# The last up group of an FFN by the seven-product form, in a fused streaming-encoder step

## The chip, the cores and the metric

The kernel runs on one core of one Trainium2 chip. The metric is device time in microseconds (us) of one execution; less is better. Engines are named as the profile names them: PE (TensorE matmul), PEld (its weight loads), DVE (VectorE), ACT (ScalarE), POOL (GpSimd) and SP (SyncE, which here only issues DMAs).

## What is computed

One layer of a hybrid streaming encoder for two groups of requests that share the weights: a convolution branch and an attention branch, mixed, and behind them a gated feed-forward network (FFN). The change touches the FFN alone. 256 prompt frames and 8 x 16 frames of running streams make 384 tokens, three tiles of 128.

```
    h2 = rmsnorm(x, norm_ffn_g)
    up = h2 @ w_up                       # (384, 2048) @ (2048, 11264)
    g_half = up[..., :D_FF]              # D_FF = 5632
    u_half = up[..., D_FF:]
    ext_f = jnp.concatenate([ffn_buf.astype(g_half.dtype), g_half], axis=1)
    gc = causal_dwconv(ext_f, ffn_dw_w, ffn_dw_b)          # 3 taps along time
    x = x + (jax.nn.silu(gc) * u_half) @ w_down            # (384, 5632) @ (5632, 2048)
    new_ffn = ext_f[:, -(FFN_CONV_W - 1):]
```

All of it is float32. TensorE works in a rounded 32-bit form (fp32r), so every operand is split into a rounded part and a rest, `hi` and `lo`, and every product is three matmuls: hi times hi, hi times lo, lo times hi.

## The kernel before

**Groups.** The 5632 columns of the FFN are cut into 11 groups of 512. "Up" of a group makes 512 gate and 512 value columns for 384 tokens from 16 chunks of 128 input rows. "Down" of a group (a down round, numbered by its group from 0) multiplies the gated result, four chunks of 128, by four panels of 512 output columns and adds the panels to `y`. `FFN_PLAN` (lines 192 to 195) is the order: up 0, then up g and down g-1 for g from 1 to 10, then down 10. So the end of the program is up 9, down 8, up 10, down 9, down 10.

**Steps.** Everything in the FFN is a list of steps. A step takes one weight tile of 128 x 1024 floats (two input chunks by 512 columns, 512 KB). SP loads it into one of five raw buffers: three tiles `raw` and two thirds of a fixed tile `raws`, in rotation (`stream_tile`, line 141). ACT casts it to `hi`, DVE subtracts to `lo` (there are three pairs of buffers), and PE multiplies. `step` (line 1228) records PE's matmuls of one step, and beside them the cast and subtraction for the step two further on. `room` counts free raw buffers; `load_ahead` issues loads while there are any.

**Two forms of up.** The direct form (`plain_up`, line 1473; `tokens`, line 1449) has 16 steps of 18 matmuls (2 chunks x 3 token tiles x 3). The seven-product form (`wino`, line 1380) multiplies two of the token tiles by 12 of the 16 chunks as a 2 x 2 x 2 block scheme with seven products in place of eight. It has 25 steps: 9 of 12 matmuls ("s" and "b"), 4 of 18 ("cg" and "cu", the four chunks outside the scheme) and 6 pairs of 9 and 6 ("t"). For each pair DVE first combines two raw tiles: three subtractions of 128 x 512 for its first step and a fourth for its second. The sums of token tiles that the scheme needs lie in `sums` and in a tile `late`, made once. `WINO` (line 196) names the groups in this form: 1 to 9. Groups 0 and 10 are direct.

**Turn and gating.** When a group's rows stand in `gr` (gate) and `ur` (value), `finish_up` (line 1307) turns them: DVE transposes 32 x 32 blocks of the three token tiles into a buffer `tb`, and 16 DMAs for each of `gr` and `ur`, 8 issued by SP and 8 by POOL, move the blocks into a tile `uT` (class `Turn`, line 1266). `tb` and `uT` exist once, so `ur` waits for `gr` to have left them. From the turned gate rows ACT makes four copies and two halo copies into `extf` and the first convolution tap, DVE the taps two and three (`sg`), and ACT applies SiLU. DVE multiplies the turned value rows by it (`uT<-uT,sg`, two halves), ACT casts them (`hi` part of `act`), DVE subtracts (`lo` part, `act<-uT,act`). `act` of a group is what its down round multiplies. The halves are halves of the 32-token blocks, so each holds a part of all four chunks of `act`.

**What sets the order.** A planner in the program's own Python keeps for each engine a time of its own (`now`) and a list of open work (`todo`). Work of the turn and gating goes into the gaps between a step's fixed instructions when its planned end is no later than the step's end plus `SLACK` (0.8 us). The instruction streams of the engines keep that order: DVE, ACT, SP and POOL each run theirs in order. `foresee` and `spare` compute numbers that nothing uses.

In the profile, line 1100 is the call through which all of these instructions of DVE, ACT, SP and POOL go, so they are told apart by tile. Lines 1376, 1377 and 1378 are the three matmuls of a product.

Of the kernel before, what the change touches and what calls it, by code (L numbers as in the profile page):

```python
# [15 lines left out]
P = 128  # L16
DM = 2048
NT = 384
# [23 lines left out]
def hybrid_step(  # L42
# [28 lines left out]
    made = [0, 0, -1]  # L71
# [136 lines left out]
    for what, g in FFN_PLAN:  # L208
# [22 lines left out]
        else:  # L231
            for cols in N_COLS:
                planned(w_down, 4 * g[0], cols, 4 * len(g))
# [872 lines left out]
    MM, HI, LO, SUM, RAWS, SLACK = 0.227, 1.05, 1.22, 0.7, 5, 0.8  # L1106
# [55 lines left out]
    def load_ahead():  # L1162
        while plan:
# [31 lines left out]
    at = [0]  # L1195
    need = []

    def foresee():
        behind = 0.0
        for what, g in FFN_PLAN:  # L1200
            if what == "up" and g in WINO:
                n = len(need)
                for kind, _ in WINO_STEPS:
                    if kind == "t":
                        need.extend([(9, 3 * SUM + LO), (6, SUM + LO)])
                    else:
                        need.append((18 if kind[0] == "c" else 12, LO))
                need[n] = (need[n][0], need[n][1] + behind)
                need[-2] = (need[-2][0], need[-2][1] + 0.7)
                need[-1] = (need[-1][0], need[-1][1] + 1.4)  # L1210
                behind = 2.1
            else:
                n, rounds, adds = (8, 2, 0.0) if what == "up" else (2 * len(g), 4, 2.1)
                for _ in range(rounds):
                    need.extend([(18, LO + behind)] + [(18, LO)] * (n - 1))
                    behind = adds
        need.extend([(18, 0.0)] * 2)

    def spare(end):
        latest, t, used = end + 9.0, end, 0.0  # L1220
        for j in range(at[0] + 2, min(at[0] + 14, len(need))):
            t += MM * need[j - 1][0]
            if j > at[0] + 2:
                used += LO if j == at[0] + 3 else need[j][1]
            latest = min(latest, t - 0.5 - used)
        return latest

    def step(mults, products):

        t = now["PE"]  # L1230
        for e in todo:
# [20 lines left out]
        if nxt:  # L1252
            work("DVE", hi_done + 0.1)
# [7 lines left out]
        for e in ("SP", "ACT", "DVE", "ACT", "SP"):  # L1261
            work(e, end + SLACK)
        at[0] += 1
        now["PE"] = end

    class Turn:

        def __init__(self, tiles, rows):
            self.tiles, self.rows = tiles, rows

        def one(self, t):
            if t == 0:
                self.tb = p_f.tile([P, 4, 4, NTT, 32], F32, tag="tb", bufs=1, name="tb")
            V.transpose(self.tb[:].rearrange("p q m t j -> p t m q j")[:, t],
                        getattr(self.tiles, self.rows)[:, t, :].rearrange("p (m q j) -> p m q j", m=4, q=4))
# [8 lines left out]
        def blocks(self):  # L1284
            return [("DVE", 0.72, 0.2, lambda t=t: self.one(t)) for t in range(NTT)]

        def moves(self):
            return [("SP", 1.4, 0.0 if a < 3 else 6.0, lambda a=a: self.move(a)) for a in range(4)]
# [18 lines left out]
    def finish_up(g, tiles, ready, both=True):  # L1307
        gt, ut = Turn(tiles, "gr"), Turn(tiles, "ur")
# [19 lines left out]
        def halves(x):  # L1328
# [246 lines left out]
```

## Time and profile before

| what | value |
|---|---|
| time, median of 3 runs | 1964.83 us (1963.3 to 1965.12) |
| the profiled execution's own time | 1964.78 us |
| span of the profile, first to last instruction | 1963.1 us |
| granted TensorE clock, mean | 0.999 |
| PE busy | 1951.5 us (99%), 9210 matmuls |
| DVE busy | 1448.3 us (74%) |
| ACT busy | 869.7 us (44%) |
| share of the chain that ended last on PE | 94% |

The page of the profile gives busy times by engine and by group of instructions. The timeline of an engine gives each instruction's start, its duration and, in brackets, how long the engine sat idle before it and what released it. A row with "x3" is three instructions that follow each other, with their time together. In a timeline a step of the direct form is 18 matmuls, and up of one group begins where the operand changes from `act` to `xg`.

### The profile page before, as it was taken

To read this page: it belongs to the slowest core of one execution; us is meant where nothing else is said; L and a number is where in the kernel's file an instruction comes from. 1 tells how busy PE (TensorE), PEld (TensorE's weight loads), DVE (VectorE), ACT (ScalarE), POOL (GpSimd) and SP (SyncE) were. 2 spreads that over 40 slices of the span, in tenths; PEclk is the share of its full clock that TensorE was granted. 3 is DMA by queue.
4 is the path that set the end of the run, shared out by engine and by line. 5 is a ranking of instruction groups with operands and counts; after the bars stand their busy time and mean duration, and the time that the engine had idled before them with its cause. 6 is when DMAs were issued, how large, how long until landed. Compare 5 with 4: busy or idle time off the path is not lost.

```text
span 1963.1 us, 25493 instructions
## 1 busy us (share of the span) xinstructions
PE 1951.5 (99%) x9210; PEld 1644.6 (84%) x9210; DVE 1448.3 (74%) x1977; ACT 869.7 (44%) x1212; POOL 150.4 (8%) x298
## 2 busy tenths in 40 slices
PE   9999999999999999999999999999999999999999
PEld 9888999888888888888888888888888888888887
DVE  4456879788764578677587878787878787878555
ACT  5535354433334523344454444454444445454442
POOL 2000011100000000000111010101010101010110
PEclk9999999999999999999999999999999999999999
DMA  6574777454444333644566666666666666666553
GB/s 186 150 183 118 215 168 154 138 143 132 131 130 128 128 126 122 197 132 140 156 218 202 198 203 201 199 207 195 207 189 211 194 209 190 216 189 215 146 163 114
DMA packets 242755, 335.86 MB, mean 171 GB/s; under 512 B 60651, under 2 KB 106406, under 8 KB 242620
## 3 DMA queue, kind: packets, MB, share of 16 engines
q1 hardware_dynamic: 235427, 324.21, 56.0%
q0 software_dynamic: 7168, 10.00, 1.9%
q8 instruction: 72, 1.18, 0.3%
q14 instruction: 56, 0.45, 0.1%
q10 hardware_dynamic: 32, 0.01, 0.0%
HBM read 309.45 MB, written 7.86 MB: 162 GB/s over the span
## 4 chain that ended last, share of the span: by engine, by line
PE 94%; DVE 4%; issue 1%; DMA 1%; ACT 1%; SPq 0%; ACTq 0%; DVEq 0%
PE bank L1377 17%; PE bank L1378 17%; PE bank L1376 16%; PE acc L314 8%; PE acc L312 8%; PE acc L313 8%; PE misc L314 4%; PE misc L313 4%; PE misc L312 4%; PE acc L307 2%; PE acc L309 2%; PE acc L308 2%; DVE lo L1100 1%; DVE raw L1100 0%; ACT hi L1100 0%
## 5 line engine op out<-in xcount | busy, mean ns | idle before, releaser
L168 DVE TENSOR_TENSOR lo<-raw,hi 128x1024 fp32r<-128x1024 f32 (+2 forms) x219 | 259.3, 1184 | 198.8 <-ACT hi L167 193.6
L167 ACT CAST hi<-raw 128x1024 fp32r<-128x1024 f32 (+2 forms) x219 | 221.7, 1012 | 396.6 <-PE misc L314 305.0
L1100 ACT CAST hi<-raw 128x1024 fp32r<-128x1024 f32 x207 | 217.4, 1050 | 327.2 <-PE bank L1378 273.3
L1100 DVE TENSOR_TENSOR lo<-raw,hi 128x1024 fp32r<-128x1024 f32 x207 | 252.4, 1221 | 114.7 <-ACT hi L1100 111.8
L1377 PE MATMUL bank<-lo,xg 128*128 128x512 f32 x696 | 271.9, 391 | 1.5 <-DVE lo L1100 1.5
L1376 PE MATMUL bank<-hi,xg 128*128 128x512 f32 x696 | 270.9, 389 | 0.0
L1378 PE MATMUL bank<-hi,xg 128*128 128x512 f32 x696 | 270.8, 389 | 0.0
L1100 ACT CAST hi<-raws 128x1024 fp32r<-128x1024 f32 x136 | 143.4, 1054 | 215.4 <-PE bank L1378 182.2
L1100 DVE TENSOR_TENSOR lo<-raws,hi 128x1024 fp32r<-128x1024 f32 x136 | 166.0, 1221 | 80.2 <-ACT hi L1100 77.8
L1376 PE MATMUL bank<-hi,act 128*128 128x512 f32 x528 | 205.4, 389 | 0.0
L1377 PE MATMUL bank<-lo,act 128*128 128x512 f32 x528 | 205.4, 389 | 0.0
L1378 PE MATMUL bank<-hi,act 128*128 128x512 f32 x528 | 205.4, 389 | 0.0
L312 PE MATMUL acc<-hi,hT 128*128 128x512 f32 (+1 forms) x512 | 193.2, 377 | 0.1
L314 PE MATMUL acc<-hi,hT 128*128 128x512 f32 (+1 forms) x512 | 190.7, 372 | 0.1
L313 PE MATMUL acc<-lo,hT 128*128 128x512 f32 (+1 forms) x512 | 190.4, 372 | 0.0
L1377 PEld LDWEIGHTS bank<-lo,xg 128*128 128x128 f32 x696 | 130.6, 188 | 32.5 <-DVE lo L1100 5.6
L829 DVE SCALAR_TENSOR_TENSOR ut<-ext,cw,ut 128x384 f32<-128x384 f32 x240 | 152.2, 634 | 6.0
L1376 PEld LDWEIGHTS bank<-hi,xg 128*128 128x128 f32 x696 | 130.7, 188 | 27.4
L1378 PEld LDWEIGHTS bank<-hi,xg 128*128 128x128 f32 x696 | 130.7, 188 | 26.7
L1100 POOL DMA_DIRECT2D uT<-tb x176 | 86.7, 500 | 862.7 <-DVE y L1100 595.7
L1376 PEld LDWEIGHTS bank<-hi,act 128*128 128x128 f32 x528 | 99.1, 188 | 20.6
L1378 PEld LDWEIGHTS bank<-hi,act 128*128 128x128 f32 x528 | 99.1, 188 | 20.5
(353 smaller groups left out, 3539.5 us busy)
## 6 DMA issues: line engine op xcount, KB each, us to landing
raw<-in_w_up_dram SPq DMA_DIRECT2D x156, 512.0 KB
raws<-in_w_up_dram SPq DMA_DIRECT2D x101, 512.0 KB
raw<-in_w_in_dram SPq DMA_DIRECT2D x96, 512.0 KB
raw<-in_w_down_dram SPq DMA_DIRECT2D x53, 512.0 KB
raws<-in_w_down_dram SPq DMA_DIRECT2D x35, 512.0 KB
raw<-in_w_in_dram SPq DMA_DIRECT2D x64, 256.0 KB
raw<-in_w_out_dram SPq DMA_DIRECT2D x32, 512.0 KB
uT<-tb SPq DMA_DIRECT2D x176, 48.0 KB
```

The source lines that it names most:

```text
L167: queued(nc.scalar.copy(hi[:, k, :o], raw[:, k, :o]), first)
L168: queued(tt(lo[:, k, :o], raw[:, k, :o], f(hi[:, k, :o]), op=ALU.subtract), first)
L307: mm(o, hi[:, kk, s], ah, start=st, stop=False)
L308: mm(o, hi[:, kk, s], al, start=False, stop=False)
L312: mm(o, ah[:, s], hi[:, kk, :n], start=st, stop=False)
L313: mm(o, ah[:, s], lo[:, kk, :n], start=False, stop=False)
L314: mm(o, al[:, s], hi[:, kk, :n], start=False, stop=sp)
L829: stt(o, v, wc, o, op0=ALU.mult, op1=ALU.add)
L1100: d = op(*args, **kw)
L1376: mm(o, ah, h[:, kk, :], start=start, stop=False, **kw)
L1377: mm(o, ah, l[:, kk, :], start=False, stop=False, **kw)
L1378: mm(o, al, h[:, kk, :], start=False, stop=stop, **kw)
```

## The change

- Group 10 goes to the seven-product form (`WINO` is 1 to 10).
- The order at the end becomes up 9, down 8 without its last panel, up 10, that panel, down 9, down 10.
- `act` of group 10 gets the buffer `G3`, which `late` holds until up 10 is done, in place of one that alternates. Its value rows are turned in a buffer of their own, the second half of `raws`; from behind the eighth-last step of up 10 on, the fifth raw buffer, which lies there, is left out of the rotation. The transposes of a token tile are queued as soon as its rows stand.
- Weight loads are held back from the last step of up 10 until the gate rows' moves are issued (`hold`).
- Behind up 10 the planner's slack is 8 us in place of 0.8, and the gating goes by halves of chunks: taps, SiLU, multiplication and split for chunks 0 and 1, then for 2 and 3. In every other group the halves are halves of chunks too, and each half's multiplication waits for its own SiLU alone.
- `foresee` and `spare` are gone.

```diff
     def stream_tile():
         made[2] += bool(banks)
+        made[2] += made[2] % 5 == 4 and made[3]
...
-    for g in range(1, 11):
+    for g in range(1, 9):
         FFN_PLAN += [("up", g), ("down", (g - 1,))]
-    FFN_PLAN += [("down", (10,))]
-    WINO = tuple(range(1, 10))
+    FFN_PLAN += [("up", 9), ("down", (8,), range(3)), ("up", 10), ("down", (8,), range(3, 4)), ("down", (9,)), ("down", (10,))]
+    WINO = tuple(range(1, 11))
...
     def load_ahead():
-        while plan:
+        while plan and not hold:
...
+    slack, hold = [0.8], []
     def step(mults, products):
         t = now["PE"]
+        if slack[0] > 1:
+            work("SP", t + 4.0)
+            work("ACT", t + 2.0)
...
-            work("DVE", hi_done + 0.1)
+            work("DVE", max(hi_done + 0.1, end - 0.5 if slack[0] > 1 else 0.0))
...
         for e in ("SP", "ACT", "DVE", "ACT", "SP"):
-            work(e, end + SLACK)
+            work(e, end + slack[0])
...
         def move(self, a):
...
+            if a == 3:
+                hold.clear()
...
-        def halves(x):
-            return x.rearrange("p m (t a j) -> p a (m t) j", t=NTT, a=4)
+        def two(x, h):
+            return x[:, 2 * h:2 * h + 2].rearrange("p m (t a j) -> p a (m t) j", t=NTT, a=4)
         def ft(h):
-            return ut.ft[:, 2 * h:2 * h + 2].rearrange("p a m t j -> p a (m t) j")
+            return ut.ft[:, :, 2 * h:2 * h + 2].rearrange("p a m t j -> p a (m t) j")
...
+        ends = [joined(2, [("DVE", 0.97, 0.2, lambda h=h: mul(h)), ("ACT", 0.83, 0.2, lambda h=h: high(h)),
+                           ("DVE", 0.97, 0.2, lambda h=h: low(h))]) for h in range(2)]
         conv = [("ACT", 0.55, 0.2, halo)]
+        for ms in ((0, 1), (2, 3)) if tb is not None else (range(4),):
+            conv += [("DVE" if w else "ACT", 0.64 if w else 0.53, 0.1, lambda w=w, m=m: tap(w, m)) for w in range(3) for m in ms]
+            for h in {m // 2 for m in ms}:
+                conv += [("ACT", 0.85, 0.2, lambda h=h: silu(h)), [ends[h]]]
...
+        if tb is not None:
+            move_u = joined(4, ut.moves() + [[out] + last])
+            move_g = joined(3, gt.moves() + copies + [[move_u, conv]])
+            return lambda rows, t, ready: chain(ready, (gt.blocks((t,)) + move_g) if rows == "gr" else
+                                                (ut.blocks((t,)) + move_u))
...
+        if g == 10:
+            turn = finish_up(g, tiles, 0.0, tb=res["raws"][:].rearrange("p x m t -> p (x m t)")[:, 1536:3072].rearrange(
+                "p (q m t j) -> p q m t j", q=4, m=4, t=NTT))
+            turns = {2: [("gr", 0)], "g": [("gr", 2)], 4: [("gr", 1), ("ur", 2), ("ur", 0), ("ur", 1)]}
...
+            if turn:
+                for x in [x for b in done for x in turns.get(b, [])]:
+                    fins.append(("NONE", 0.0, lambda x=x: turn(*x, max(now["DVE"], now["ACT"]) + 0.3)))
+                if j == len(steps) - 8:
+                    made[3] = 1
+                    room[0] -= 1
+                if j == len(steps) - 1:
+                    hold.append(1)
...
+            if g[0] >= 9 or g[0] == 8 and only[0][0]:
+                slack[0] = 8
+            while g[0] == 10 and any(todo.values()):
+                for e in todo:
+                    work(e, 1e6)
```

Three places show what that does to the order of instructions.

**DVE, group 9's gating.** `uT<-uT,sg` and `act<-uT,act` are the four gating instructions of group 9; `lo` is a step's subtraction, `raw` and `raws` rows without `lo` are combinations of weight tiles. Before, they stand in the third and fourth step of the direct up 10:

```order
L1100 TENSOR_TENSOR lo<-raw,hi 128x1024
L1100 TENSOR_TENSOR uT<-uT,sg 128x768 x2
L1100 TENSOR_TENSOR lo<-raw,hi 128x1024
L1100 TENSOR_TENSOR act_14915<-uT,act_14915 128x2x12x32 x2
L1100 TENSOR_TENSOR lo<-raw,hi 128x1024
```

In the changed kernel they stand among the pairs of the seven-product up 10; the first of these rows follows the `lo` of the first pair's first step:

```order
L1101 TENSOR_TENSOR uT<-uT,sg 128x4x192
L1101 TENSOR_TENSOR lo<-raws,hi 128x1024
L1101 TENSOR_TENSOR uT<-uT,sg 128x4x192
L1101 TENSOR_TENSOR raw<-raw 128x512 x3
L1101 TENSOR_TENSOR lo<-raw,hi 128x1024
L1101 TENSOR_TENSOR raw<-raw 128x512
L1101 TENSOR_TENSOR lo<-raw,hi 128x1024 x2
L1101 TENSOR_TENSOR act_14955<-uT,act_14955 128x4x6x32
L1101 TENSOR_TENSOR raw<-raws,raw 128x512
```

The last `act` of group 9 stands one pair further on, also between the last `lo` of a step and the three subtractions of the next pair.

**DVE, behind up 10.** `ur` and `gr` rows end the up group, `tb<-gr` and `raws<-ur` are the transposes, `y` rows the additions of a finished panel. Before, the gate rows were turned in the middle of the direct up 10 and the value rows one by one in the first steps of down 9:

```order
L1100 TENSOR_TENSOR lo<-raws,hi 128x1024
L1100 STREAM_TRANSPOSE tb<-ur 128x4x4x32
L1100 SCALAR_TENSOR_TENSOR sg<-extf,fw,sg 128x384
L1100 TENSOR_TENSOR lo<-raw,hi 128x1024
L1100 STREAM_TRANSPOSE tb<-ur 128x4x4x32
```

Now all six stand together between the `lo` of the third step behind the group and that of the fourth:

```order
L1101 SCALAR_TENSOR_TENSOR ur<-bank,rs_6845,ur 128x512
L1101 SCALAR_TENSOR_TENSOR gr<-bank,rs_6845,ur 128x512
L1101 SCALAR_TENSOR_TENSOR ur<-bank,rs_6845,ur 128x512
L1101 TENSOR_TENSOR lo<-raw,hi 128x1024
L1101 STREAM_TRANSPOSE tb<-gr 128x4x4x32 x3
L1101 STREAM_TRANSPOSE raws<-ur 128x4x4x32 x3
L1101 TENSOR_TENSOR lo<-raws,hi 128x1024
L1101 TENSOR_TENSOR y<-bank,y 128x512 x3
```

**SP, behind up 10.** `uT` rows are moves of turned blocks, the others loads of the steps of the down rounds. Before, loads stood between the moves of `gr` in up 10, and the moves of `ur` stood together but for the last two:

```order
L1100 DMA uT<-tb 32x384 x6
L1100 DMA raw<-in_w_down_dram 128x2x512
L1100 DMA uT<-tb 32x384 x2
L1100 DMA raws<-in_w_down_dram 128x2x512 x2
```

Now all 8 moves of `gr` go ahead of the seventh load behind up 10, and the moves of `ur` have the loads of the eleventh and twelfth step between them:

```order
L1101 DMA uT<-tb 32x384 x8
L1101 DMA raw<-in_w_down_dram 128x2x512
L1101 DMA raws<-in_w_down_dram 128x2x512
L1101 DMA raw<-in_w_down_dram 128x2x512 x2
L1101 DMA uT<-raws 32x384 x2
L1101 DMA raw<-in_w_down_dram 128x2x512
L1101 DMA uT<-raws 32x384 x4
L1101 DMA raws<-in_w_down_dram 128x2x512
L1101 DMA uT<-raws 32x384 x2
```

More of the change, by code (lines that the diff above doesn't have):

```diff
@@ L207, in hybrid_step @@
         planned(w_out, 0, cols, 16)
-    for what, g in FFN_PLAN:
+    for what, g, *only in FFN_PLAN:
         if what == "up" and g in WINO:
@@ new lines, in finish_up @@
+        last = list(ends)
+        if tb is not None:
[3 more added lines that the diff above has]
+                                                (ut.blocks((t,)) + move_u))
+        move_u = joined(2, ut.moves() + [[out] + last])
+        chain(ready, gt.blocks() + gt.moves() + [[copies + [[move_u, conv]], ut.blocks() + move_u if both else []]])
@@ L1476, in plain_up, with down @@
         tokens([(grouped(xg), 16, up_rows(tiles, "ur"), lambda: then[0](now["ACT"] + 0.3))])
-    def down(gs):
+    def down(gs, only=range(4)):
         def tiles(k):
@@ L1493, in add @@
             return ev
[L1495 removed]
+        js = [(tiles, 4 * len(gs), add(n), lambda: None) for n in only]
         for j in js:
```

100 lines of the change are left out of this document (31 added, 69 removed).

## The prediction

> **What bounds the kernel.** The page comes first: the busy times, and the shares of the chain that ended last.
>
> ```profile
> PE   1951.5 (99%) x9210; PEld 1644.6 (84%) x9210; DVE 1448.3 (74%) x1977; ACT 869.7 (44%) x1212; POOL 150.4 (8%) x298
> PE 94%; DVE 4%; issue 1%; DMA 1%; ACT 1%; SPq 0%; ACTq 0%; DVEq 0%
> ```
>
> PE is the bound, and no other engine is near it on average. Whether it is limited by matmuls or by waits is answered by PE's own waits, from the FFN's start to the end:
>
> ```profile
> PE bank L1377 <- DVE lo L1100: 1.9, 10, 0.3
> ```
>
> Ten waits for a `lo`, 1.9 us together: one or so for each seven-product group. So time is the number of matmuls times their pitch, and a gain must come from fewer of them. PE's timeline gives it, here at the first matmul of up 9, of down 8, of up 10 and of down 9:
>
> ```profile
> 1733.43 0.39 PE L1376 MATMUL bank<-hi,xg 128*128 128x512 f32 x1
> ...
> 1795.09 0.39 PE L1376 MATMUL bank<-hi,act 128*128 128x512 f32 x1
> ...
> 1827.73 0.39 PE L1376 MATMUL bank<-hi,xg 128*128 128x512 f32 x1
> ...
> 1893.01 0.39 PE L1376 MATMUL bank<-hi,act 128*128 128x512 f32 x1
> ```
>
> Up 9 (seven products) took 1795.09 - 1733.43 = 61.66 us, up 10 (direct) 1893.01 - 1827.73 = 65.28. The difference, 3.62 us, is what the exchange is worth if group 10 runs as group 9 does.
>
> **Fewer matmuls, and one wait more.** The direct form has 16 x 18 = 288 matmuls, 65.28 / 288 = 0.2267 us each; the other has 9 x 12 + 4 x 18 + 6 x 15 = 270. The 18 that go are worth 18 x 0.2267 = 4.08 us. But 270 x 0.2267 are 61.2, not 61.66: group 9 loses 0.43 in one place.
>
> ```profile
> 1761.31 0.39 PE L1376 MATMUL bank<-hi,xg 128*128 128x512 f32 x1
> 1761.86 0.50 PE L1377 MATMUL bank<-lo,xg 128*128 128x512 f32 x1 [0.16 <-DVE lo L1100]
> 1762.20 0.39 PE L1378 MATMUL bank<-hi,xg 128*128 128x512 f32 x1
> ```
>
> The two distances, 0.55 and 0.34, are 0.32 and 0.11 over the pitch. DVE's timeline shows why:
>
> ```profile
> 1756.52 1.23 DVE L1100 TENSOR_TENSOR lo<-raws,hi 128x1024 fp32r<-128x1024 f32 x1 [1.14 <-ACT hi L1100]
> 1757.66 0.95 DVE L1100 TENSOR_TENSOR act<-uT,act 128x768 fp32r<-128x768 f32 x1
> 1758.53 2.14 DVE L1100 TENSOR_TENSOR raw<-raw 128x512 f32<-128x512 f32 x3
> 1760.58 1.22 DVE L1100 TENSOR_TENSOR lo<-raws,hi 128x1024 fp32r<-128x1024 f32 x1
> ...
> 1764.80 0.95 DVE L1100 TENSOR_TENSOR act<-uT,act 128x768 fp32r<-128x768 f32 x1
> ...
> 1769.46 2.56 DVE L1100 TENSOR_TENSOR lo<-raws,hi 128x1024 fp32r<-128x1024 f32 x2
> 1772.79 2.15 DVE L1100 TENSOR_TENSOR raw<-raw 128x512 f32<-128x512 f32 x3 [0.77 <-DMA raw<-in_w_up_dram]
> ```
>
> Behind the `lo` at 1756.52 come a gating instruction (0.95), three combinations and the late `lo` (ends 1761.80). In the new up 10 the order puts `uT<-uT,sg` at that point, with the same 0.95. So I charge the wait again: +0.43.
>
> Group 10's DVE carries all four gating instructions of group 9 among its pairs, two more than group 9's carried of group 8 (1757.66 and 1764.80). Bounds: nothing, if both fall into idle time, and 2 x 0.95 = 1.9 if neither does. The first falls ahead of the `lo` with 1.14 idle; the last falls ahead of the combinations with 0.77 idle for a weight load and leaves 0.2, which the next `lo` has to spare. I take nothing. In groups 2 to 9 a gating instruction moves forward by one `lo`; the one ahead of the late `lo` stays, in kind, so their waits stay. The new strides keep the number of elements, so I keep the durations; scaled to 768 elements, the nearest rows (a `lo` of 1024 in 1.22, three taps of 384 in 1.67, both quoted here) give 0.92 and 1.11 for the 0.95, at most 0.16 more, which costs only where a `lo` is late: 0.16 in each of ten groups at the worst, 1.6.
>
> **Four raw buffers for five.** The first loads of the rounds behind up 10 go out one step later. The tightest, by group 9's rows, is that for the third step: its buffer is free when the `lo` at 1789.61 ends, and the cast stands at 1796.03.
>
> ```profile
> 1789.61 1.23 DVE L1100 TENSOR_TENSOR lo<-raw,hi 128x1024 fp32r<-128x1024 f32 x1 [0.41 <-ACT hi L1100]
> ...
> 1796.03 1.04 ACT L1100 CAST hi<-raw 128x1024 fp32r<-128x1024 f32 x1
> ...
> 1764.91 4.42 SPq L1100 DMA_DIRECT2D raw<-in_w_up_dram  x2
> ```
>
> The second of the two loads in the last row was out at 1769.33 and DVE took its data at 1772.79: 3.5 us. 1790.84 + 0.4 + 3.5 = 1794.7, 1.3 ahead of the cast. I take nothing; if such a load took twice 3.5, it would be 2.2 late, and that is the other end.
>
> **The turn and the gating of group 10**, now behind the group, must end before down 10. I walk it from t = 0 at the first matmul behind up 10, with group 9's rows (t = 0 at 1795.09); a step is 18 x 0.2267 = 4.08 us.
>
> ```profile
> 1800.16 2.35 DVE L1100 TENSOR_TENSOR lo<-raw,hi 128x1024 fp32r<-128x1024 f32 x2
> 1802.43 1.89 DVE L1100 STREAM_TRANSPOSE tb<-gr 128x512 f32<-128x512 f32 x3
> ...
> 1940.81 2.05 DVE L1100 TENSOR_TENSOR y<-bank,y 128x512 f32<-128x512 f32 x3 [0.41 <-PE bank L1378]
> ```
>
> The third step's `lo` ends at t = 6.2. Six transposes follow, 3.8, to 10.0 (the gate's to 8.1); the fourth step's `lo` ends at 11.2 and is wanted by its second matmul, at 12.5. Margin 1.3. (The value rows' transposes write to `raws`; for that I take the same row.)
>
> ```profile
> 1811.01 2.41 SPq L1100 DMA_DIRECT2D uT<-tb  x4
> ...
> 1804.89 3.96 POOL L1100 DMA_DIRECT2D uT<-tb  x8 [72.35 <-DVE y L1100]
> ...
> 1901.90 3.91 POOL L1100 DMA_DIRECT2D uT<-tb  x8 [29.18 <-DVE tb L1100]
> uT<-tb POOLq DMA_DIRECT2D x48, 48.0 KB, 3.0
> ...
> 1816.64 1.76 ACT L1100 COPY extf<-uT 128x384 f32<-128x384 f32 x4
> 1818.43 0.31 ACT L1100 COPY extf<-extf 128x120 f32<-128x120 f32 x1
> 1818.64 0.25 ACT L1100 COPY extf<-sfT 128x64 f32<-128x64 f32 x1
> ...
> 1820.72 2.51 ACT L1100 ACTIVATE sg<-extf,col,fw 128x384 f32<-128x384 f32 x4
> 1942.17 1.05 ACT L1100 CAST hi<-raw 128x1024 fp32r<-128x1024 f32 x1 [3.03 <-PE bank L1378]
> ...
> 1826.07 1.67 DVE L1100 SCALAR_TENSOR_TENSOR sg<-extf,fw,sg 128x384 f32<-128x384 f32 x3
> ...
> 1915.83 1.82 DVE L1100 TENSOR_TENSOR uT<-uT,sg 128x768 f32<-128x768 f32 x2
> ```
>
> SP's eight gate moves take 4.9, to 13.0; 3.0 to landing, 16.0. ACT's order has copies, halos and a tap ahead of the seventh step's cast: 17.7, cast 18.8 (its load, held until 13.0, is there at 16.9), `lo` 20.1, wanted 24.7: **margin 4.6**. The value moves: two at 17.7; then SP's queue has a load that waits for that `lo` (20.1), four moves, a load that waits for the next `lo` (23.0, behind three taps), two moves at 24.6; landed 27.6. The first half's product 28.6, three taps, and the tenth step's `lo`, which stands behind them on DVE, 31.5, wanted 36.9: **margin 5.4**. The first half of `act` is whole at 32.4 and wanted at 40.8. The second half's product stands behind the additions of the panel that ends at 32.6 and the eleventh step's `lo` (35.1): 36.0; the twelfth's `lo`, whose cast waits for PE until 36.7, ends 39.2; `act` whole at 40.1, wanted at 44.9: **margin 4.8**. Every term has cover, so the turn costs nothing.
>
> **Sum.** -4.08 + 0.43 = -3.65, beside 3.62 from the two spans: 1964.78 - 3.6 = **1961.2**. The profiled execution is 0.05 under the median of the runs shown, so that goes for the median too. 0.2% is 3.93 us, about what a measurement of this kernel can tell from no change; the forecast falls just short of it.
>
> **Rivals.**
>
> *More comes off.* In two groups a second wait stood where a gating instruction goes away:
>
> ```profile
> 1105.25 0.69 DVE L1100 TENSOR_TENSOR raws<-raw,raws 128x512 f32<-128x512 f32 x1 [0.87 <-DMA raws<-in_w_up_dram]
> ...
> 1107.88 0.39 PE L1376 MATMUL bank<-hi,late 128*128 128x512 f32 x1
> 1108.59 0.50 PE L1377 MATMUL bank<-lo,late 128*128 128x512 f32 x1 [0.32 <-DVE lo L1100]
> 1108.93 0.40 PE L1378 MATMUL bank<-hi,diff_lo 128*128 128x512 f32 x1
> ...
> 1485.92 0.39 PE L1376 MATMUL bank<-hi,late 128*128 128x512 f32 x1
> 1486.27 0.50 PE L1377 MATMUL bank<-lo,late 128*128 128x512 f32 x1
> ```
>
> Over the pitch the first loses 0.48 + 0.11, the second 0.12. If DVE's work was the cause, -0.7: 1960.5, and 1960.1 without group 10's own wait. Against it: DVE sat idle 0.87 for the load there. But the forecast lies only 0.3 from the bound of 0.2%, and the runs before spread over 1.8 us.
>
> *DVE's pairs run over.* Both added gating instructions push the `lo` of their steps: up to +1.9, 1963.1. For it: from 1757.66 to 1774 DVE's timeline has one idle stretch, the 0.77. Against: each stands at an idle place.
>
> *Slower: late moves hold DVE's and ACT's queues.* The value rows can't leave before the gate's copies are made, so a delay x in each of the two landings counts twice at the tenth step's `lo`: a stall of 2x - 5.4. It eats the gain at x = 4.5 and is slower by 0.2% from x = 6.5, that is 9.5 us to landing for 3.0; x = 9 gives a stall of 12.6 and 1973.8. For it: held loads and moves go out in one burst. Against: 9.5 is three times the row.
>
> The Trainium skill speaks against this part in two places. "SBUF — State Buffer", section "SBUF: two separate sides", says that DMAs issued from GpSimd can starve while VectorE holds a port that both share, and the section on the bandwidth-pool intuition has one go from 620 to 3100 ns. With 3.1 for each of POOL's eight, x would be 20.9, the stall 36 and the time 1998, an estimate from that page. By that rule the rows above would differ; the trace does not agree: eight took 3.96 and 3.91 with DVE at additions and `lo` beside them, so it gets 0.01 of the chance for slower. "TensorE: Matmul & The Clock Gate", section "What's actually happening", has PE at half rate after an idle window of some 3.4 us, so that a long stall would cost more than itself; no run here shows it (the granted clock was 0.999).
>
> That up 10 isn't changed as said is excluded: PE's order has 18 rows fewer.
>
> **Chances.** Forecast 0.46; more comes off, beyond 3.93 us, 0.32; pairs run over or a part of the margins, still under 0.2% either way, 0.10; slower 0.12. So faster 0.32, same 0.56, slower 0.12. The range takes in the first rival and some of the runs' spread below (1959.5), and above the 1.9 of the pairs and most of the 2.2 of the buffers (1965.0).
>
> **What would show it.** Up 10 from its first `xg` matmul to the next `act` takes 61.7; one wait on PE some 28 us into it, 0.4 in all; no wait on PE in the 18 steps behind it. The copies into `extf` about 16 us behind the group, `uT<-uT,sg` at 28, the last `act` at 40. Wrong it would be made by a PE wait behind `act`, by a cast that waits for a weight load behind up 10, or by groups 2 to 9 that run other than before.

## Result and profile after

| | before | after |
|---|---|---|
| median of 21 runs | 1964.82 us (1963.18 to 1966.19) | 1961.20 us (1959.25 to 1963.03) |
| after / before | | 0.9982, 95% interval 0.9975 to 0.9989 |
| profiled execution, its span | 1964.78 us, 1963.1 us | 1961.57 us, 1959.9 us |

The change brings 3.6 us, as forecast. From the page after, the same two lines as those of before:

```profile
PE 1948.2 (99%) x9192; PEld 1640.7 (84%) x9192; DVE 1480.1 (76%) x2016; ACT 879.0 (45%) x1220; POOL 150.9 (8%) x298
PE 93%; DVE 4%; issue 1%; DMA 1%; ACT 1%; SPq 0%; ACTq 0%; DVEq 0%
```

PE has 18 matmuls fewer (9210 before) and is still the bound at 99%; DVE has 39 instructions more. PE's waits in the FFN are eleven now, one for each seven-product group and one more, in the same sum:

```profile
PE bank L1357 <- DVE lo L1101: 1.9, 11, 0.3
```

PE's timeline at the first matmul of up 9, of down 8, of up 10 and of the panel behind it, with the wait inside up 10:

```profile
1734.12 0.39 PE L1356 MATMUL bank<-hi,xg 128*128 128x512 f32 x1
...
1795.77 0.39 PE L1356 MATMUL bank<-hi,act 128*128 128x512 f32 x1
...
1820.25 0.39 PE L1356 MATMUL bank<-hi,xg 128*128 128x512 f32 x1
...
1848.13 0.39 PE L1356 MATMUL bank<-hi,xg 128*128 128x512 f32 x1
1848.68 0.50 PE L1357 MATMUL bank<-lo,xg 128*128 128x512 f32 x1 [0.16 <-DVE lo L1101]
1849.01 0.39 PE L1358 MATMUL bank<-hi,xg 128*128 128x512 f32 x1
...
1881.91 0.39 PE L1356 MATMUL bank<-hi,act 128*128 128x512 f32 x1
```

Up 9 takes 1795.77 - 1734.12 = 61.65 us and up 10 now 1881.91 - 1820.25 = 61.66, for 65.28. The one wait in up 10 comes 28 us into it and costs 0.32 + 0.11. From 1881.91 on, PE runs 324 matmuls with no gap to its last, at 1955.12.

One trap lies in these rows: up 9 starts 0.69 us later than before (1733.43), though only the order of the gating changes ahead of it. 0.48 of that is there already at the wait in up 1 (1006.10 for 1005.62), 0.21 come in groups 1 to 8. Up 9 starts between 1732.3 and 1735.4 us in the traces of the experiments that leave everything ahead of it as it is.

Part of that scatter has a cause in the traces. At about 353 us PE stands 2.5 us, and behind it the granted clock is 0.50 for 3.4 us in twelve of the fourteen traces, before and after among them; the first 100 matmuls from there on take 13.9 to 14.2 us. In the other two, e4 and e8, the clock stays at 1.00 and they take 12.6.

So I compare **one stretch**, from up 9's first matmul to PE's end (the last matmul's start and one pitch): 224.86 us before, 221.23 after, a difference of 3.63. This stretch repeats within 0.02 us between kernels that should not differ in it (before and e3; after, e5 and e7; e1 and e10), where their medians differ by up to 0.9, and the experiments are read by it. That the median after meets the forecast to the tenth is therefore partly luck; that the stretch is 3.63 shorter is not.

### The profile page after: what moved, and what is told of

It reads as the page before. It is cut to its first block, busy times and chain, and to the rows that moved or that the text cites. A ratio compares the mean times of both kernels' runs of the same rounds, so it can differ in the third digit from the quotient of the medians.

```text
span 1959.9 us, 25541 instructions
## 1 busy us (share of the span) xinstructions
PE 1948.2 (99%) x9192; PEld 1640.7 (84%) x9192; DVE 1480.1 (76%) x2016; ACT 879.0 (45%) x1220; POOL 150.9 (8%) x298
## 4 chain that ended last, share of the span: by engine, by line
PE 93%; DVE 4%; issue 1%; DMA 1%; ACT 1%; SPq 0%; ACTq 0%; DVEq 0%
PE bank L1357 16%; PE bank L1358 16%; PE bank L1356 16%; PE acc L315 8%; PE acc L313 8%; PE acc L314 8%; PE misc L315 4%; PE misc L313 4%; PE misc L314 4%; PE acc L308 2%; PE acc L309 2%; PE acc L310 2%; DVE lo L1101 1%; DVE raw L1101 1%; ACT hi L1101 1%
## 5 line engine op out<-in xcount | busy, mean ns | idle before, releaser
L1101 ACT CAST hi<-raw 128x1024 fp32r<-128x1024 f32 x215 | 225.8, 1050 | 322.8 <-PE bank L1358 273.6
L1101 DVE TENSOR_TENSOR lo<-raw,hi 128x1024 fp32r<-128x1024 f32 x215 | 262.3, 1222 | 90.6 <-ACT hi L1101 87.2
L1357 PE MATMUL bank<-lo,xg 128*128 128x512 f32 x656 | 256.6, 391 | 1.7 <-DVE lo L1101 1.7
L1358 PE MATMUL bank<-hi,xg 128*128 128x512 f32 x656 | 255.4, 389 | 0.0
L1356 PE MATMUL bank<-hi,xg 128*128 128x512 f32 x656 | 255.3, 389 | 0.0
L1357 PEld LDWEIGHTS bank<-lo,xg 128*128 128x128 f32 x656 | 123.1, 188 | 31.6 <-DVE lo L1101 6.2
L1101 POOL DMA_DIRECT2D uT<-tb x168 | 82.7, 501 | 855.4 <-DVE y L1101 652.2
L1356 PEld LDWEIGHTS bank<-hi,xg 128*128 128x128 f32 x656 | 123.1, 188 | 25.7
L1358 PEld LDWEIGHTS bank<-hi,xg 128*128 128x128 f32 x656 | 123.1, 188 | 25.3
L1356 PEld LDWEIGHTS bank<-hi,act 128*128 128x128 f32 x528 | 99.1, 188 | 20.6
L1357 PEld LDWEIGHTS bank<-lo,act 128*128 128x128 f32 x528 | 99.1, 188 | 20.6
```

Source lines behind the costliest of these rows:

```text
L1101: d = op(*args, **kw)
L1356: mm(o, ah, h[:, kk, :], start=start, stop=False, **kw)
L1357: mm(o, ah, l[:, kk, :], start=False, stop=False, **kw)
L1358: mm(o, al, h[:, kk, :], start=False, stop=stop, **kw)
```

## Experiments

| | what is different | median us | stretch us |
|---|---|---|---|
| before | | 1964.8 | 224.86 |
| after | | 1961.2 | 221.23 |
| e1 | after, one gating instruction earlier in each group | 1956.9 | 220.33 |
| e2 | after, combinations behind the late `lo` | 1965.2 | 221.90 |
| e3 | after's order, up 10 direct | 1964.8 | 224.85 |
| e4 | after, no panel behind up 10 | 1965.3 | 224.30 |
| e5 | after, no hold of loads | 1960.8 | 221.23 |
| e6 | after, no own buffer | 1968.3 | 229.94 |
| e7 | after, group 10's gating by whole chunks | 1960.4 | 221.25 |
| e8 | after, all moves of group 10 by POOL | 1962.3 | 223.10 |
| e9 | before, with e1's edit | 1961.2 | 224.40 |
| e10 | after, with e1's edit, no hold, whole chunks | 1956.1 | 220.33 |

**e3: the panel and the halves of chunks alone.**

```diff
-    WINO = tuple(range(1, 11))
+    WINO = tuple(range(1, 10))
```

> The order of the steps as in the changed kernel (one panel of the eighth down round behind up 10, halves of chunks in the gating, `act` of group 10 in its own place), but up 10 in the direct form, five raw buffers, no hold. Theory (the whole gain is the 18 matmuls less the one wait; moving the panel and halving by chunks are free): from up 9's first matmul to PE's end 224.9 us as before, 1964.8 us. Rival (moving the panel takes or brings something by itself): off 1964.8 by over 1 us.

Measured 1964.83 us, 1.0002 of before (0.9993 to 1.0011), stretch 224.85 for 224.86. Moving the panel and regrouping the gating are free and bring nothing by themselves.

**e1: the wait.** The gating instruction in question is placed one `lo` earlier (`quiet` holds the step's number in steps 8 and 9 of a group):

```diff
-            work("DVE", max(hi_done + 0.1, end - 0.5 if slack[0] > 1 else 0.0))
+            work("DVE", hi_done + (1.2 if quiet == [8] else -9.0) if quiet else max(hi_done + 0.1, end - 0.5 if slack[0] > 1 else 0.0))
...
         for e in ("SP", "ACT", "DVE", "ACT", "SP"):
-            work(e, end + slack[0])
+            if e != "DVE" or not quiet:
+                work(e, end + slack[0])
+        if quiet == [9]:
+            work("DVE", now["DVE"] + 1.0)
```

> The changed kernel, with one DVE instruction of the gating moved ahead by one `lo` in each of the ten seven-product groups: it now stands ahead of the `lo` in front of which DVE sat idle 1.14 us, and no longer between that `lo` and the three combinations. Theory (the one wait of each group is DVE's chain, and the gating instruction of 0.95 us in it is what is too much): 0.95 is more than the 0.42 of the wait, so it goes in all ten groups, 10 x 0.42 = 4.2 us: 1957.0 us, and up 10 takes 61.2 us for 61.66. Rival (the wait is set by the cast or by the weight load, and DVE only follows): the wait stays, 1961.2 us.

Measured 1956.89 us, 0.996 of before (0.9948 to 0.9973): 4.3 us under the changed kernel. DVE's timeline of this kernel at the place in up 9 of which the prediction showed the rows of before:

```profile
1751.05 1.22 DVE L1101 TENSOR_TENSOR lo<-raw,hi 128x1024 fp32r<-128x1024 f32 x1
1752.19 0.95 DVE L1101 TENSOR_TENSOR act<-uT,act 128x768 fp32r<-128x768 f32 x1
1753.42 1.23 DVE L1101 TENSOR_TENSOR lo<-raws,hi 128x1024 fp32r<-128x1024 f32 x1 [0.28 <-ACT hi L1101]
1754.56 2.14 DVE L1101 TENSOR_TENSOR raw<-raw 128x512 f32<-128x512 f32 x3
1756.62 1.22 DVE L1101 TENSOR_TENSOR lo<-raws,hi 128x1024 fp32r<-128x1024 f32 x1
```

The 0.95 us of the gating instruction now fill most of the 1.14 idle ahead of the `lo`, 0.28 are left, and the combinations follow at once. The late `lo` ends at 1757.84, and PE's pitch stays whole there; PE's waits for `lo` in the FFN fall from eleven to none that the view lists. The stretch, which holds two such groups, is 0.90 shorter. (In up 10 the edit also brings one `act<-uT,act` forward, past two `lo`.) So the wait was DVE's chain, and the place of one instruction in it made the wait, not the amount of DVE's work.

**e2: the other cure, which fails.** The combinations go behind the late `lo`:

```diff
-        if staged:
+        if staged and not quiet:
             combine(staged[0])
...
             room[0] += 1
+        if staged and quiet:
+            combine(staged[0])
```

> The changed kernel, with the three combinations of the second pair behind the late `lo` and no longer ahead of it, in each of the ten seven-product groups; the gating instruction stays where it was. Theory (DVE's chain): the late `lo` comes 2.1 us earlier, the wait of 0.42 goes in ten groups: 1957.0 us. What comes later is the cast of the pair's first weight tile, by some 1 us; by rows of group 9 its `lo` would then end some 0.8 us ahead of PE, so no new wait. Rival: that margin isn't there, a new wait of up to 0.5 comes at the pair, 1957 to 1962 us. Rival (cast or load set the wait): 1961.2 us.

Measured 1965.2 us, 0.9999 of before (0.999 to 1.0008): the whole gain is gone. DVE's timeline in up 9:

```profile
1762.90 1.23 DVE L1101 TENSOR_TENSOR lo<-raws,hi 128x1024 fp32r<-128x1024 f32 x1 [0.63 <-ACT hi L1101]
1764.05 2.86 DVE L1101 TENSOR_TENSOR raw<-raw 128x512 f32<-128x512 f32 x4
1767.43 2.36 DVE L1101 TENSOR_TENSOR lo<-raw,hi 128x1024 fp32r<-128x1024 f32 x2 [0.52 <-ACT hi L1101]
1769.71 2.14 DVE L1101 TENSOR_TENSOR raws<-raws 128x512 f32<-128x512 f32 x3
```

The old wait goes, as the theory said, and the margin counted at the pair is there: its first `lo` ends at 1768.6, and PE wants it at 1769.3 (up 9 began at 1737.10). But DVE now idles twice, 0.63 for the cast ahead of the late `lo` and 0.52 for the next cast, which needs the combinations: combine, cast and subtract stand in series. So the next pair's combinations start only at 1769.71, and the `lo` behind these, that of the step after the pair, ends at 1772.99 and is 0.46 late. The loss falls one `lo` further on than I had looked. PE's waits for `lo` rise from 1.9 us to 4.3, at 14 places:

```profile
PE bank L1360 <- DVE lo L1101: 4.3, 14, 1.0
```

**e9: e1's edit in the kernel before.** The edit is the same, with `now["DVE"] + 1.2` as the bound in step 8 and no forced placing.

> The kernel before (up 10 direct), with the gating instruction one `lo` earlier in its nine seven-product groups, as in the first experiment. Theory (the wait is one thing, the exchange of matmuls another, and they add): 9 x 0.42 = 3.8 us go, and with them the second waits of groups 2 and 6 (0.59 and 0.34) if DVE's chain made these too: 1960.1 to 1961.0 us. Against the first experiment's 1956.9 the exchange is then worth 18 matmuls, 4.1 us, with no wait taken off. Rival (the gain of the first experiment came with the changed gating by halves of chunks): 1964.8 us, or the exchange is worth clearly less or more than 4.1.

Measured 1961.24 us, 0.9978 of before (0.9968 to 0.9987). That is 0.2 above the range's upper end: short waits of 0.07 to 0.29 stay in groups 1, 2 and 6. (The 0.34 of the expectation for group 6 is a whole distance between two matmuls; over the pitch that group loses 0.12 + 0.11.) The clean number is the difference to e1 in the stretch: 224.40 - 220.33 = 4.07, against 18 x 0.2267 = 4.08. **The exchange of matmuls is worth exactly its matmuls**; the 0.44 between that and the 3.63 of the change is the one added wait.

**e4, e11 and e12: the cover.**

```diff
-    for g in range(1, 9):
+    for g in range(1, 11):
         FFN_PLAN += [("up", g), ("down", (g - 1,))]
-    FFN_PLAN += [("up", 9), ("down", (8,), range(3)), ("up", 10), ("down", (8,), range(3, 4)), ("down", (9,)), ("down", (10,))]
+    FFN_PLAN += [("down", (10,))]
```

> The changed kernel with the whole of down 8 ahead of up 10, so that 8 steps (32.6 us) and not 12 (48.9 us) lie between up 10 and down 10. Theory (the turn and the gating need their measured 34.9 us for the first half of `act` and some 39 for the second, if both go ahead of DVE's additions): PE waits 2.2 to 3 us for `act` in front of down 10, 1963.4 to 1964.2 us. Rival (no cover is needed, the panel could have stayed): 1961.2 us. Rival (the turn takes much longer when squeezed): 1964.8 us or more.

Median 1965.33 us, 1.0 of before (0.9991 to 1.0009): by the median the whole gain goes, and more than the theory said. (The 12 steps and 48.9 us of the expectation are a slip: of the 324 matmuls behind up 10, 180 stand ahead of down 10 in the changed kernel, 10 steps or 40.8 us, as the prediction has it; the panel is 2 steps of cover.) The profiled execution (1962.84) has the wait in front of down 10 that was forecast. PE's timeline:

```profile
1920.73 0.39 PE L1358 MATMUL bank<-hi,act 128*128 128x512 f32 x1
1921.04 0.50 PE L1356 MATMUL bank<-hi,act 128*128 128x512 f32 x1
1921.38 0.40 PE L1357 MATMUL bank<-lo,act 128*128 128x512 f32 x1
1924.12 0.50 PE L1358 MATMUL bank<-hi,act 128*128 128x512 f32 x1 [2.34 <-DVE act L1101]
1924.45 0.39 PE L1356 MATMUL bank<-hi,act 128*128 128x512 f32 x1
```

1921.38 to 1924.12 is 2.51 over the pitch, and the stretch is 3.07 longer than the changed kernel's. That gives 1964.3, just above what was expected, and not the median of 1965.3: of eleven runs five lay between 1962.7 and 1963.9 and five between 1965.3 and 1968.0 (one was far off, at 5932 us). So I ran it twice more for its trace.

> The fourth experiment once more, for its profile: there PE stood 2.5 us at one matmul and its times lay in two clusters, about 1963 and about 1966.5 us. Theory (in some executions the wait gets long enough that PE runs slower behind it, as in the sixth experiment, where 14 matmuls behind a wait of 5.8 us took 0.43 us each): an execution of the upper cluster shows matmuls of 0.43 us behind the wait, one of the lower cluster shows none. Rival (the clusters have nothing to do with the wait): pitch 0.227 behind the wait at any time.

> The same once more, since one execution falls into one cluster only: matmuls of 0.43 us behind the wait if its time is about 1966.5 us, none if it is about 1963 us; by the rival none in either.

They took 1966.22 and 1966.06 us. From the third trace, PE behind the same wait:

```profile
1922.82 0.50 PE L1356 MATMUL bank<-hi,act 128*128 128x512 f32 x1 [0.34 <-ACT act L1101]
1923.16 0.40 PE L1357 MATMUL bank<-lo,act 128*128 128x512 f32 x1
1925.90 0.50 PE L1358 MATMUL bank<-hi,act 128*128 128x512 f32 x1 [2.34 <-DVE act L1101]
1926.23 0.40 PE L1356 MATMUL bank<-hi,act 128*128 128x512 f32 x1
...
1927.44 0.63 PE L1358 MATMUL bank<-hi,act 128*128 128x512 f32 x1
1927.86 0.63 PE L1356 MATMUL bank<-hi,act 128*128 128x512 f32 x1
```

In both, PE waited 0.4 us more ahead of the long wait than in e4, and then eight matmuls stand 0.43 us apart, not 0.227 (in e11 at once behind the wait, in this trace 1.5 us later). The granted clock there is 0.52 in e11 (1926.3 to 1929.8 us) and 0.51 in e12 (1927.4 to 1930.8); in e4 it is 1.00 behind the wait. The two stretches are 226.13 and 226.12, 1.8 longer than e4's.

So both executions of the upper cluster show what the theory wanted, and the one profiled of the lower shows none. But it is only about half of the distance between them: the other 1.5 of some 3.3 us lie ahead of up 9 (it starts at 1732.34 in e4, at 1733.89 and 1733.74 in e11 and e12), and there e4 is the trace whose clock was not halved at 353 us. What decides in an execution whether the clock is halved behind such a wait is not shown.

**e6: the own buffer.** The value rows go back into the gate's transposed tile, and the fifth raw buffer stays:

```diff
-            self.tiles, self.rows, self.tb = tiles, rows, tb
+            self.tiles, self.rows, self.tb = tiles, rows, tb or None
...
-            turn = finish_up(g, tiles, 0.0, tb=res["raws"][:].rearrange("p x m t -> p (x m t)")[:, 1536:3072].rearrange(
-                "p (q m t j) -> p q m t j", q=4, m=4, t=NTT))
+            turn = finish_up(g, tiles, 0.0, tb=0)
...
-                if j == len(steps) - 8:
-                    made[3] = 1
-                    room[0] -= 1
```

> The changed kernel without the own buffer: the value rows are transposed into the same tile as the gate's, and all five raw buffers stay. Theory: DVE's value transposes then wait for the landing of the gate's moves (+14.8 behind up 10), with the fourth step's `lo` behind them in DVE's queue: it ends at about +17.8 for +11 and is wanted at +12.5, so PE stands 5 to 6 us: 1966.5 us, and the wait is for `lo`. Rival (the buffer isn't needed, the turn has cover): 1961.2 us.

Measured 1968.32 us, 1.0018 of before (1.0008 to 1.0027). DVE's timeline behind up 10, and PE's:

```profile
1888.07 1.89 DVE L1101 STREAM_TRANSPOSE tb<-gr 128x512 f32<-128x512 f32 x3
1897.08 1.90 DVE L1101 STREAM_TRANSPOSE tb<-ur 128x512 f32<-128x512 f32 x3 [7.12 <-DMA uT<-tb]
1898.90 1.18 DVE L1101 TENSOR_TENSOR lo<-raw,hi 128x1024 fp32r<-128x1024 f32 x1
```

```profile
1894.10 0.39 PE L1356 MATMUL bank<-hi,act 128*128 128x512 f32 x1
1900.14 0.80 PE L1357 MATMUL bank<-lo,act 128*128 128x512 f32 x1 [5.65 <-DVE lo L1101]
1900.73 0.63 PE L1358 MATMUL bank<-hi,act 128*128 128x512 f32 x1
...
1905.42 0.63 PE L1357 MATMUL bank<-lo,act 128*128 128x512 f32 x1
1905.85 0.51 PE L1358 MATMUL bank<-hi,act 128*128 128x512 f32 x1
1906.20 0.39 PE L1356 MATMUL bank<-hi,act 128*128 128x512 f32 x1
```

The transposes stand 7.12 us in DVE's queue, the `lo` behind them ends 18.2 us behind up 10 (expected 17.8) and PE waits 5.8 over its pitch, as the theory said. Then comes what it didn't hold: 14 matmuls some 0.43 us apart, which take another 2.9 us: 5.8 + 2.9 = 8.7, and the stretch is 8.71 longer. The view of windows gives the granted clock (the third number from the end) for these 14 and for what follows:

```profile
1900.14:1906.20 6.06, 6.06 (x15) 4.77 (x15) 4.70 (x6) 0.00 (x0) 4.92 (x10) 0.51 0.81 226
1906.20:1912.00 5.80, 5.80 (x27) 4.83 (x26) 4.19 (x6) 2.50 (x3) 0.00 (x0) 1.00 0.58 202
```

So the slow matmuls are PE at half its clock.

**e5 and e8: hold and late moves.** e5 takes out the hold, the first piece here; e8 sends all moves of group 10 by POOL, the second:

```diff
-                if j == len(steps) - 1:
-                    hold.append(1)
...
-                (G if q % 2 else S).dma_start(
+                (G if q % 2 or hold or slack[0] > 1 else S).dma_start(
```

> The changed kernel without the hold: the weight loads behind up 10 stand in SP's queue where their buffers come free, and not behind the gate's moves. In the changed kernel four held loads of 512 KB go out from 1895.08 to 1897.4, and POOL's value moves, issued from 1897.5 on, take 7.2 us to landing for the 3.0 of before. Theory (the moves wait in the DMA engines behind that burst): without it POOL's value moves land in 3 to 4.5 us, the first product `uT<-uT,sg` starts at +27 to +28.5 behind up 10 for +30.0, no stall, 1961.2 us. Rival (POOL's queue is slow beside DVE's work, whatever the loads do): 7 us to landing, product at +30. Rival (without the hold the gate's moves come late and the turn doesn't fit): PE waits for a `lo` or for `act`, over 1962.5 us.

> The changed kernel, with all 16 moves of each of group 10's two tiles on POOL's queue, none on SP's; SP's loads then go out when their buffers come free, with no burst. Theory (POOL takes 0.5 us to issue a move and a move lands in some 3 us where no burst is ahead of it): gate tile whole at +19, value tile at +30.5 to +31.5, the tenth step's `lo` at +35 to +36 for a want of +36.9: no stall, 1961.2 us. Rival (POOL's moves land in 7 us beside DVE's work, burst or not): value tile at +34.5 to +39, that `lo` 1.7 to 6 us late, PE waits for it: 1963 to 1967 us.

The transfers of the changed kernel, then of e5, 1895 to 1915 us (issues, KB each, median us to landing):

```profile
uT<-raws POOLq DMA_DIRECT2D x8, 48.0 KB, 7.2
```

```profile
uT<-raws POOLq DMA_DIRECT2D x8, 48.0 KB, 3.0
```

The issuing takes POOL the same in both, eight in 3.91 us. DVE is busy for 80% of the time from the first issue to the last landing in the changed kernel and for 82% in e5. In e8, where POOL issues all 16 and SP's loads are spread out, the landing takes 3.3 (DVE 66% busy). So POOL is not slowed by DVE's work here; the moves lie behind the burst of four held 512 KB loads. The second half of e5's theory fails: its first product starts at 1911.78, 29.8 behind up 10 (1881.94), no earlier than with the hold. Not POOL's moves but the last two of SP's end the turn, and without the hold these stand in SP's queue behind the loads until 1907.46. The hold costs about as much at the landing as it saves in the queue (the last move is out 26.2 behind up 10 with it and 26.7 without, and lands 3.8 and 3.2 later): 1960.75 us, 0.9978 of before (0.9968 to 0.9987), stretch 221.23 with and without it.

e8 measured 1962.34 us, 0.9987 of before (0.9978 to 0.9996), and fell between the theories: no landing of 7 us, yet a wait of PE, at a place that I had not walked for it. ACT's timeline in e8:

```profile
1900.47 0.53 ACT L1101 COPY extf<-uT 128x384 f32<-128x384 f32 x1 [3.10 <-DMA uT<-tb]
1902.78 0.52 ACT L1101 COPY extf<-uT 128x384 f32<-128x384 f32 x1 [1.78 <-DMA uT<-tb]
...
1903.82 0.71 ACT L1101 ACTIVATE sg<-extf,col,fw 128x384 f32<-128x384 f32 x1
1904.43 1.03 ACT L1101 CAST hi<-raw 128x1024 fp32r<-128x1024 f32 x1
```

The gate's last part comes to ACT 7 us later than in the changed kernel, and the seventh step's cast stands behind its copy. Some 4 of the 7 are the issue of all 16 moves by one engine (the last is out at 17.2 behind up 10 for 13.2). The rest is landing: the last of these moves took 5.0, with two 512 KB loads issued among them (1894.90 and 1896.04). The seventh step's `lo` ends at 1906.73, 25.8 behind up 10; the prediction had it wanted at 24.7, and PE waits 1.1 there. The tenth step's ends 38.4 behind, for 36.9 + 1.1 = 38.0, and PE waits another 0.3; at the eleventh step it loses 0.2 more. Together that is 1.7 of the 1.87 by which the stretch is longer. **The margins of the walk are real**: once they are used up, PE pays.

**e7: halves of chunks in group 10.**

```diff
-        for ms in ((0, 1), (2, 3)) if tb is not None else (range(4),):
+        for ms in (range(4),):
```

> The changed kernel, with group 10's gating not by halves: all taps of the four chunks ahead of both products, which then stand behind the additions of the panel that ends at +32.6. Theory (from the trace of the changed kernel, where the value lands at +30): the first half of `act` ends at about +41.2, wanted at +40.8, the second at +43.4, wanted at +44.9: PE waits 0.3 to 1 us for `act`, 1961.5 to 1962.2 us. Rival (the halves are what makes the turn fit, several us at stake): over 1963.5 us. Rival (no difference): 1961.2 us, no wait at down 10's first step.

Measured 1960.35 us, 0.9978 of before (0.9969 to 0.9987), stretch 221.25, no wait behind up 10. The expected 0.3 to 1 us did not come. I had let the panel's additions begin where they do in the changed kernel, 35.4 behind up 10 (1917.30); they stood there only because DVE was busy until then. Here DVE was free, they came as their panel ended, and the first product started at 34.0. The order by halves buys nothing here.

**e10: what is left when both are dropped.** e1's edit, e5's and e7's in one.

> The changed kernel with the gating instruction one `lo` earlier (first experiment), without the hold and with group 10's gating by whole chunks. Theory (neither the hold nor the halves carries anything, and the three edits don't touch one another): the first experiment's time, 1956.9 us, no wait on PE behind up 10. Rival (the hold or the halves is needed once the other is gone): PE waits for `act` or a `lo` behind up 10, 1957.5 to 1960 us.

Measured 1956.09 us, 0.9955 of before (0.9942 to 0.9968), stretch 220.33 as in e1. This is the fastest version, some 9 us under the kernel before, of which a little less than half is the change and the rest the place of one instruction; it is simpler than e1, and no slower. In its trace PE still waits at the late `lo` of groups 3 and 7 (0.55 and 0.39): there the combinations ahead of it had waited 0.90 and 0.74 us for a weight load. Where the gating instruction is out of the chain, the load is the next thing in it.

## Why the prediction was right, step by step

**18 matmuls, -4.08: right.** Up 10 takes what up 9 takes, and with the waits gone on both sides the difference is 4.07 (e1 and e9).

**One wait more, +0.43: right, with its cause.** It came at 28 us into up 10 with 0.32 + 0.11, and e1 shows that the gating instruction in that place makes it.

**Gating of group 9 among the pairs, 0: right.** DVE's timeline after, at the last of the two added instructions:

```profile
1857.61 1.23 DVE L1101 TENSOR_TENSOR lo<-raw,hi 128x1024 fp32r<-128x1024 f32 x1
1858.75 0.95 DVE L1101 TENSOR_TENSOR act<-uT,act 128x768 fp32r<-128x768 f32 x1
1859.62 0.69 DVE L1101 TENSOR_TENSOR raws<-raw,raws 128x512 f32<-128x512 f32 x1
```

No idle time for a load is left, the pair's `lo` moves back, and PE doesn't wait: 61.66 us for 61.65. So the rival by which the pairs run over did not happen.

**Four raw buffers for five, 0: right.** The third step's cast stands at 1882.85, 0.9 behind up 10 as in group 9, with ACT busy up to it, so it did not wait for its load.

**Groups 2 to 9 unchanged: right in the sum.** From the wait in up 1 to up 9 it is 728.02 us for 727.81. The single waits differ: group 2's second wait is 0.34 after for 0.59 before, group 6's 0.55 for 0.23. That groups 2 to 9 run other than before was named as a sign of error, but these differences are not the change's. In the nine traces of kernels that have the changed order there (after, e3 to e8, e11, e12), group 2's second wait is anything from 0 to 0.69, group 6's from 0.26 to 0.77, and the whole from 727.31 to 728.21. So the rival by which more comes off did not happen, and the waits that it was built on vary from one execution to the next. Its idea was half right: where the gating instruction moves, waits go (e1), but the change left the instruction that makes them.

**The turn: right that it is free, wrong in one size.** Times behind up 10's end:

| | predicted | measured | wanted |
|---|---|---|---|
| transposes end | 10.0 | 9.9 | |
| fourth step's `lo` ends | 11.2 | 11.0 | 12.5 |
| seventh step's `lo` ends | 20.1 | 19.9 | 24.7 |
| value rows landed | 27.6 | 30.0 | |
| tenth step's `lo` ends | 31.5 | 34.1 | 36.9 |
| first half of `act` whole | 32.4 | 34.9 | 40.8 |
| `act` whole | 40.1 | 41.3 | 44.9 |

The step that was off is the landing of the value rows. SP's timeline after, the view of SP's waits from 1904 to 1908 us (us in total, times, longest), and ACT's and DVE's timelines:

```profile
1902.24 2.66 SPq L1101 DMA_DIRECT2D uT<-raws  x4
1906.49 0.37 SPq L1101 DMA_DIRECT2D raws<-in_w_down_dram  x1
1906.98 1.14 SPq L1101 DMA_DIRECT2D uT<-raws  x2
```

```profile
SPq L1101 <- DMA raw<-in_w_down_dram: 1.5, 1, 1.5
```

```profile
1899.50 1.05 ACT L1101 CAST hi<-raw 128x1024 fp32r<-128x1024 f32 x1 [1.08 <-DMA raw<-in_w_down_dram]
```

```profile
1911.95 0.96 DVE L1101 TENSOR_TENSOR uT<-uT,sg 128x768 f32<-128x768 f32 x1 [2.92 <-DMA uT<-raws]
```

SP's queue stood until 1906.49 and not until the `lo` that I had walked (1904.83), so the last moves were out 1.6 us later than forecast. They landed 3.8 us after, for the 3.0 of an unloaded queue. 1.6 + 0.8 = 2.4, nearly half of the margin of 5.4 at the tenth step; 2.8 were left. What SP stood for was the landing of an earlier weight load: by the trace's semaphores the last of the four held ones, out at 1896.99 and landed at 1906.42, 9.4 us later. The same load in e5, without a burst, held nothing there. The cast at 1899.50 did wait for a held load, which I had named as a sign of error; it had cover. The rival of late moves was thus the one with something in it. Its burst is real: it more than doubled the landing of POOL's moves (e5), which did not end the turn, and it delayed the last moves of SP, which did. Its price stayed inside the cover.

Of the two rules set against this part, the first has no support here. "SBUF — State Buffer" in the Trainium skill (section "SBUF: two separate sides") has DMAs issued from GpSimd starve while VectorE runs an operation in a two-port mode. DVE's rows beside POOL's moves are additions, subtractions, transposes and taps, and the copy that the page names as its example is not among them; the prediction left that condition out. The moves landed in 3.0 and 3.3 us (medians of the value rows, e5 and e8) with no burst ahead.

The other bears on this case, and the prediction was wrong that no run shows it. "TensorE: Matmul & The Clock Gate" in the Trainium skill (section "What's actually happening") has PE at half rate after an idle window of some 3.4 us. The half rate is shown: 0.43 us for a matmul at a granted clock of 0.51 behind a wait of 5.8 (e6). The trace of the kernel before has it too, behind the idle time of 2.50 us at 353 us:

```profile
352.40:355.80 3.40, 3.39 (x23) 2.97 (x24) 1.68 (x11) 3.05 (x7) 1.12 (x2) 0.50 1.08 333
```

So an idle time shorter than the page's window was enough, in most executions. The mean of 0.999 that the prediction quotes hides 3.4 us of half clock.

**The parts, by what they are worth.** The panel behind up 10 (e4) and the own buffer (e6) carry the gain: without either it is gone. The hold (e5) and the halves (e7) carry none of it, singly or together (e10).

## What to carry to other kernels

On a kernel where one engine is 99% busy, price an exchange by its instruction count times the measured pitch, and check it on one stretch of that engine's timeline between two fixed points, since whole runs differ by more than such a gain. For a wait that recurs in each round, look at the waited-for engine for an idle time just ahead of the late instruction's chain: moving one instruction into it gave more here (4.3 us) than the whole change (3.6). Before a late chain is squeezed, walk it against the moments when its results are wanted, step by step, on each engine's queue; as long as the margin holds it costs nothing, and beyond it PE waits. Behind a wait of 2.5 us or more there was in most executions a penalty on top, of 1.3 to 2.9 us at half clock; behind waits of up to 1.1 us (e2, e8) there was none.

## What was not expected of the hardware

- PE's clock after a wait. 5.8 us of waiting cost 14 matmuls at 0.43 us for 0.227 (2.9 us more, granted clock 0.51, e6). A wait of 2.5 us cost eight such matmuls (some 1.7 us) in e11 and e12, in e12 only 1.5 us after the wait was over, and none in e4. In e11 and e12 0.5 us of waiting went ahead of it, in e4 0.2; but the wait of 2.5 us at 353 us, the same in all fourteen traces, halved the clock in twelve of them and not in two, so one wait can go either way. The profile's mean granted clock hardly shows it: 0.997 in e6, 0.998 in e11 and e12, 0.999 after.
- POOL's 48 KB moves inside SBUF landed in 3.0 us (median, e5) without a burst ahead and in 7.2 us (after; 6.9 in e7, both the value rows) when four loads of 512 KB had been issued just ahead of them. The last of these loads itself took 9.4 us to land.
